# A hybrid decoder layer on one core: modulation rows reduced in one pass over 2048 weights instead of two passes over 1024, with their buffers in pools of their own

## The chip, the core and the metric

The kernel runs on one core of a Trainium2 chip. The metric is the device time of one launch in microseconds. Time before: 1536.57 us, the median of three runs (1535.98 to 1537.61).

Five engines work side by side, each through its own instruction list in order: PE (TensorE) multiplies matrices, DVE (VectorE) and ACT (ScalarE) work on elements, POOL (GpSimd) starts some loads, SP (SyncE) starts nearly all of them. An instruction that waits holds up everything behind it on its engine.

## The reference, cut to what matters

One layer, 256 positions, width 2048, all in float32:

```python
mod = (silu(c) @ ada_w + ada_b)                       # 2048 x 12288 weights, one row of c
sh1, sc1, g1, sh2, sc2, g2 = split(mod, 6)
h = rms_norm(x, norm1_g) * (1 + sc1) + sh1
u, lru_gate, q, k, v, mix_gates = split(h @ w_in + b_in, SPLITS)
y_lru  = rg_lru(causal_conv(u)) * gelu(lru_gate)
y_attn = sliding_window_attention(q, k, v, sinks)
merged = sigmoid(gA) * (y_lru @ w_lru_out) + sigmoid(gB) * (y_attn @ w_attn_out)
x = x + g1 * (merged @ w_o)
h2 = rms_norm(x, norm2_g) * (1 + sc2) + sh2
gate, up = split(h2 @ w_ffn_in, 2)
x = x + g2 * ((silu(gate) * up) @ w_ffn_out)
out = rms_norm(x, final_g)
```

The change concerns the first line: six vectors of 2048 numbers, the *modulations*, each number the product of the row silu(c) with one column of ada_w.

## The kernel before

**The products.** All large products are made by `Item`s in one long list. An item is one 512 KB piece of weights (128 x 1024). Its weights are loaded by SP into a tile `raw` (L313), ACT rounds them to a high part `hi` (L330), DVE subtracts that from `raw` to get the low part `lo` (L342), and PE makes twelve matmuls of 512 columns from them (L382 to L384: high by high, low of the weights by high, high by low of the activations). There are 650 items. `step(i)` writes the instructions for one item: it issues the load of item i+5, the `hi` of item i+3, the `lo` of item i+2 and then the matmuls of item i. There are three buffers for `lo` (N_LO = 3), so the `lo` of item i+2 can start only when PE has done with the `lo` of item i-1, and PE never has more than three items ready.

**The order of the work.** Items run slab by slab: 116 items for the input projection in three pieces (`wi`), then the branch gates (`wgl`), the recurrent branch's output projection (`wl`, items 148 to 179), the other gates (`wga`), attention's output projection (`wa`, items 212 to 243), the output projection (`wo`, items 244 to 275, eight to a slab), then the feed-forward layer (`fg`, `fu`, `f..`, `pf..`). Between the items stand two kinds of smaller work. *Posts* take a slab's sums out of PSUM. *Sides* are generators that a small cost model (`run_sides`, with `charge` and a modelled `clock`) advances while it reckons that DVE and ACT have time: the modulations (`ada`), the norm of the activations (`hmod`), and the two mixers (`mix`: the recurrent unit `lru` and `attention`, four groups each). A side is also advanced at once, whatever the cost model says, where its result is needed: `of` calls `force` until the wanted part of the mixers' result stands, and `ada_to(*ms)` makes all remaining columns of the named modulations. What is written at such a place stands in DVE's list as one block.

**The modulations before.** `crow` holds silu(c) on every partition, in two tiles of 1024. For each block of 128 modulation numbers there is a row tile of 2048 weights to each of 128 partitions, loaded in two halves of 512 KB (`aw`, L503). One DVE instruction (L532, a multiply with a sum along the row) reduces each half; the second half starts from the sum of the first. There are 95 such blocks (the 96th is made by PE at the start), 190 loads and 190 passes. `Halves` holds the loads: two buffers of its own (N_ADA), and further spare tiles from the common pool `bp`, up to five (N_SPARE), where the mixers leave room. The blocks are taken in the order scale 1 and shift 1, gate 1 (m = 2), scale 2 (m = 4), shift 2 (m = 3), gate 2 (m = 5). Before the last `wo` slab, `load_rows(3)` calls `ada_to(3, 4)`; gate 2 may be made as late as the fifth slab of the feed-forward layer, where `all_modulations` calls `ada_to(5)`.

**Buffers.** The common pool `bp` has 37 tiles of 4 KB a partition: 25 counted as `b4` room, 8 for the activations `h`, 2 for `aw`, 2 for `crow`. All temporaries come from it: the mixers' tiles, `lw` (the recurrent unit's weights), and the feed-forward layer's `wx`, `wy` and `v`, which belong to its quads (seven products in place of eight).

Of the kernel before, what the change touches and what calls it, by code (L numbers as in the profile page):

```python
# [9 lines left out]
F32 = mybir.dt.float32  # L10
# [32 lines left out]
AHEAD, N_HI, N_LO, N_ADA, N_B4 = 6, 4, 3, 2, 25  # L43

N_H, N_C = 8, 2
# [32 lines left out]
N_SPARE = 5  # L78

# [4 lines left out]
def hybrid_layer(  # L84
# [11 lines left out]
    dp = ctx.enter_context(tc.tile_pool(name="dp", bufs=1, space=bass.MemoryType.DRAM))  # L96

# [72 lines left out]
    crow = [bp.tile([P, CH], F32, tag="b4", name=f"crow{j}") for j in range(N_C)]  # L170

    def crow_of(i):
        return crow[i // 2][:, i % 2 * 512:(i % 2 + 1) * 512]
# [253 lines left out]
    def seven(loads, block, by_k, act, bank, begin, end, post=None):  # L427
# [24 lines left out]
        def second(i):  # L452
# [4 lines left out]
            y = bp.tile([P, CH], F32, tag="b4", name="wy")  # L457
# [27 lines left out]
    class Halves:  # L485


        def __init__(self, srcs):
            self.srcs, self.got, self.n, self.own = srcs, [], 0, 0
            self.spare, self.limit, self.ahead = lambda: False, len(srcs), AHEAD_T  # L490

        def fetch(self):
            while self.n < min(len(self.srcs), self.limit) and clock["dma"] < clock["pe"] + self.ahead:
# [11 lines left out]
                self.got.append((t, kind, load_time(CH)))  # L505
# [4 lines left out]
        def take(self):  # L510
            t, kind, _ = self.got.pop(0)
            if kind == "own":
                self.own -= 1
            else:
                free(b4=1)
# [4 lines left out]
    def ada_cols(todo, halves):  # L520

        yield 0, 0
        for group in todo:
            for j in range(2):
                for m, kt in group:
                    v = V_ADA + m * NK + kt
                    dst = modc[:, m, kt:kt + 1]
                    if not halves.got:
# [1219 lines left out]
```

## Time and profile before

| what | value |
|---|---|
| median of three runs | 1536.57 us (1535.98 to 1537.61) |
| profiled execution: span from its first to its last instruction | 1534.3 us |
| its own time, taken as the span and 2.3 us around it (1536.57 less 1534.3) | 1536.6 us |
| PE busy | 1519.6 us, 99% of the span |
| DVE busy | 1365.7 us, 89% |
| ACT busy | 880.3 us, 57% |
| mean granted TensorE clock | 0.998 |
| DVE passes over modulation rows, L532 | 190, 241.6 us busy (120.5 + 121.1) |
| bytes moved | 444.58 MB, mean 290 GB/s |

How to read it: each engine's busy time is set against the span. Where one engine is busy nearly all the time, the span is that engine's work and its idle time; what another engine does shows in the time only as idle time of the first. In the views of instructions, a row gives start, duration, engine, line, operation, the output tile and the inputs by name, the size, and in brackets the idle time of the engine just before it with what ended it. Matmuls overlap, so PE's pace is read from the distance between two starts, not from a row's duration. "L342" is a line of the kernel before.

### The profile page before, as it was taken

The page shows a single profiled execution, that of the slowest core. Times are in us where ns is not written, and L with a number is a line of the kernel's source. Part 1 is how long each engine was busy: PE and PEld are TensorE (multiplying, and loading weights), DVE is VectorE, ACT ScalarE, POOL GpSimd, SP SyncE. Part 2 cuts the span into 40 slices and gives each one's busy share as a digit, 9 for nine tenths or more (in the row PEclk, how much of TensorE's full clock was granted, in tenths as well). Part 3 has the DMA queues.
Part 4 walks back from the last instruction along what each step waited for, and adds up shares of the span by engine and source line. Part 5 has one row for each costly group of instructions (what it writes and reads, how often), then busy time and mean ns, then how long its engine had stood idle before and what let it go on. Part 6 is the DMA issues. An engine that isn't in the chain of part 4 may idle for free.

```text
span 1534.3 us, 20203 instructions
## 1 busy us (share of the span) xinstructions
PE 1519.6 (99%) x6851; PEld 1247.3 (81%) x6851; DVE 1365.7 (89%) x1835; ACT 880.3 (57%) x1142; POOL 163.1 (11%) x232
## 2 busy tenths in 40 slices
PE   8999999999999999999999999999999999999997
PEld 5888888888888787888888878888888888888886
DVE  7999999888898887988988899999999999888988
ACT  4654444886964445434445656656566556664664
POOL 0000000000000000000002231034212122321200
PEclk9999999999999999999999999999999999999999
DMA  9999998656787888999999998589988879989983
GB/s 370 377 346 363 348 314 298 210 182 220 239 278 238 280 316 277 362 329 337 375 374 355 335 334 272 162 250 335 278 270 248 268 244 305 281 257 297 274 270 124
DMA packets 138296, 444.58 MB, mean 290 GB/s; under 512 B 16048, under 2 KB 16208, under 8 KB 138192
## 3 DMA queue, kind: packets, MB, share of 16 engines
q1 hardware_dynamic: 112912, 384.02, 70.6%
q0 software_dynamic: 24992, 58.75, 16.0%
q8 instruction: 53, 0.87, 0.2%
q10 hardware_dynamic: 288, 0.52, 0.1%
q14 instruction: 51, 0.42, 0.1%
HBM read 439.02 MB, written 4.21 MB: 289 GB/s over the span
## 4 chain that ended last, share of the span: by engine, by line
PE 92%; DMA 4%; DVE 2%; issue 1%; ACT 1%; SPq 0%; DVEq 0%; ACTq 0%
PE pf L1391 10%; PE f L384 6%; PE f L383 6%; PE f L382 6%; PE wi L383 6%; PE wi L382 6%; PE wi L384 6%; PE wgl L383 2%; PE wl L382 2%; PE wl L384 2%; PE wga L384 2%; PE wga L382 2%; PE wl L383 2%; PE wgl L384 2%; PE wo L383 2%; PE wga L383 2%
## 5 line engine op out<-in xcount | busy, mean ns | idle before, releaser
L330 ACT CAST hi<-raw 128x1024 fp32r<-128x1024 f32 (+1 forms) x540 | 532.1, 996 | 420.3 <-PE wi L384 89.8
L342 DVE TENSOR_TENSOR lo<-raw,hi 128x1024 fp32r<-128x1024 f32 (+1 forms) x540 | 612.0, 1149 | 82.6 <-issue 38.3
L383 PE MATMUL wi<-lo,h 128*128 128x512 f32 x432 | 168.9, 391 | 2.0 <-DVE lo L342 2.0
L382 PE MATMUL wi<-hi,h 128*128 128x512 f32 x432 | 170.6, 395 | 0.0
L384 PE MATMUL wi<-hi,h 128*128 128x512 f32 x432 | 168.8, 391 | 0.0
L382 PE MATMUL f<-hi,h 128*128 128x512 f32 x406 | 158.8, 391 | 0.0
L383 PE MATMUL f<-lo,h 128*128 128x512 f32 x406 | 158.2, 390 | 0.0
L384 PE MATMUL f<-hi,h 128*128 128x512 f32 x406 | 158.1, 389 | 0.0
L532 DVE CUSTOM_DVE_ANT_0 aw<-aw,crow,vec 128x1024 f32<-128x1024 f32 x95 | 120.5, 1277 | 3.4 <-DMA aw<-in_ada_t_dram 3.3
L532 DVE CUSTOM_DVE_ANT_0 aw<-aw,crow,modc 128x1024 f32<-128x1024 f32 x95 | 121.1, 1278 | 1.0 <-DMA aw<-in_ada_t_dram 0.9
L330 ACT CAST hi<-wy 128x1024 fp32r<-128x1024 f32 x55 | 58.0, 1055 | 73.7 <-PE f L384 31.7
L383 PEld LDWEIGHTS wi<-lo,h 128*128 128x128 f32 x432 | 81.6, 189 | 19.7 <-DVE lo L342 2.8
L384 PEld LDWEIGHTS wi<-hi,h 128*128 128x128 f32 x432 | 81.5, 189 | 17.1
L342 DVE TENSOR_TENSOR lo<-wx,hi 128x1024 fp32r<-128x1024 f32 x55 | 67.2, 1222 | 31.5 <-issue 27.6
L382 PEld LDWEIGHTS wi<-hi,h 128*128 128x128 f32 x432 | 81.5, 189 | 16.7 <-ACT acc L611 0.2
L330 ACT CAST hi<-wx 128x1024 fp32r<-128x1024 f32 x55 | 58.0, 1055 | 63.0 <-PE pf L1391 24.0
L383 PEld LDWEIGHTS f<-lo,h 128*128 128x128 f32 x406 | 76.3, 188 | 15.9 <-DVE lo L342 0.3
L384 PEld LDWEIGHTS f<-hi,h 128*128 128x128 f32 x406 | 76.2, 188 | 15.8
L382 PEld LDWEIGHTS f<-hi,h 128*128 128x128 f32 x406 | 76.2, 188 | 15.6
L447 POOL DMA_DIRECT2D wx<-in_w_f_dram x78 | 69.7, 967 | 86.2 <-DMA wx<-in_w_f_dram 84.8
L443 POOL DMA_DIRECT2D wx<-in_w_f_dram x78 | 45.0, 636 | 278.7 <-DVE lo L342 94.6
L342 DVE TENSOR_TENSOR lo<-wy,hi 128x1024 fp32r<-128x1024 f32 x55 | 67.2, 1222 | 6.9 <-ACT hi L330 4.2
(347 smaller groups left out, 3088.6 us busy)
## 6 DMA issues: line engine op xcount, KB each, us to landing
aw<-in_ada_t_dram SPq DMA_DIRECT2D x190, 512.0 KB, 7.2
raw<-in_w_in_dram SPq DMA_DIRECT2D x164, 512.0 KB, 5.4
raw<-in_w_f_dram SPq DMA_DIRECT2D x137, 512.0 KB, 6.7
wx<-in_w_f_dram POOLq DMA_DIRECT2D x156, 256.0 KB, 8.2
raw<-in_w_f2a_dram SPq DMA_DIRECT2D x36, 512.0 KB, 6.1
raw<-in_w_lru_dram SPq DMA_DIRECT2D x32, 512.0 KB, 4.4
raw<-in_w_att_dram SPq DMA_DIRECT2D x32, 512.0 KB, 5.8
raw<-in_w_o_dram SPq DMA_DIRECT2D x32, 512.0 KB, 8.3
```

The costliest lines, as they stand in the source:

```text
L330: nc.scalar.copy(hi[:, cs], live[i][0][:, cs])
L342: nc.vector.tensor_tensor(lo[:, cs], raw[:, cs], f32(hi[:, cs]), op=ALU.subtract)
L382: nc.tensor.matmul(ps, lhsT=lh, rhs=rh, start=start, stop=False, skip_group_check=True)
L383: nc.tensor.matmul(ps, lhsT=lh, rhs=rl, start=False, stop=False, skip_group_check=True)
L384: nc.tensor.matmul(ps, lhsT=ll, rhs=rh, start=False, stop=stop, skip_group_check=True)
L443: nc.gpsimd.dma_start(x[:, j * 512:(j + 1) * 512], block(0, 1))
L447: nc.gpsimd.dma_start(got["x"][:, j * 512:(j + 1) * 512], block(j, j), accum_op=ALU.add)
L532: nc.vector.tensor_tensor_reduce(out=r, in0=r, in1=crow[j], op0=ALU.mult, op1=ALU.add, scale=1.0, scalar=dst if j else vec[:, v:v + 1], ac ...
L1391: nc.tensor.matmul(bank(t, n), lhsT=l[:, rows(t)], rhs=w[:, c0:c0 + 512], start=kt == 0 and k == 0, stop=kt == (EARLY - 2 if (t, n) == (1, ...
```

## The change

- `crow` becomes one tile of 2048. A modulation row is loaded whole, 1 MB in one transfer, and reduced by one DVE instruction of 2048 elements. 95 loads and 95 passes take the place of 190 and 190.
- The rows have tiles of 8 KB a partition. A pool `rows` holds three (one is `crow`, two are for rows), and a pool `early` one more row until the third piece of the input projection begins. Spare tiles of the common pool are no longer used, so at most three rows, then two, are loaded ahead, where before it was up to seven halves. The common pool shrinks from 37 to 29 tiles.
- When the third piece begins, `early` is closed, and `lw` (two tiles for the recurrent unit's weights) is opened in its place.
- When all modulations are made, `lw` and `rows` are closed, and a pool `late` of eight 4 KB tiles is opened in their place. The quads' `wx`, `wy` and `v`, and some tiles of the last feed-forward slabs, come from it. Since the program text that uses `late` must stand behind the last row, `load_rows(3)` now calls `ada_to(3, 4, 5)`: all of gate 2 is made before the last `wo` slab.
- The mixers get less room, and the cost model sees other costs, so the sides are placed elsewhere.

The core of the diff:

```diff
-AHEAD, N_HI, N_LO, N_ADA, N_B4 = 6, 4, 3, 2, 25
+AHEAD, N_HI, N_LO, N_ADA, N_B4 = 6, 4, 3, 2, 21
-N_H, N_C = 8, 2
+N_H, N_EARLY = 8, 1
-N_SPARE = 5
...
-    bp = ctx.enter_context(tc.tile_pool(name="bp", bufs=N_B4 + N_H + N_ADA + N_C))
+    bp = ctx.enter_context(tc.tile_pool(name="bp", bufs=N_B4 + N_H))
...
+    def open_pool(kind, bufs):
+        guard = tc.tile_pool(name=kind, bufs=bufs, side="right", reuse_waits="tile")
...
+    open_pool("rows", N_ADA + 1)
+    open_pool("early", N_EARLY)
...
-    class Halves:
+    class Rows:
         def __init__(self, srcs):
-            self.srcs, self.got, self.n, self.own = srcs, [], 0, 0
-            self.spare, self.limit, self.ahead = lambda: False, len(srcs), AHEAD_T
+            self.srcs, self.got, self.n = srcs, [], 0
+            self.most = {"rows": N_ADA, "early": N_EARLY}
+            self.limit, self.ahead = len(srcs), AHEAD_T
         def fetch(self):
-                if self.own < N_ADA:
-                    t = bp.tile([P, CH], F32, tag="b4", name=f"aw{self.n}")
-                    self.own += 1
-                    kind = "own"
-                elif self.spare():
-                    t = b4(f"aw{self.n}", F32, (CH,))
-                    kind = "b4"
-                else:
+                kind = next((k for k, n in self.most.items() if n > 0), None)
+                if kind is None:
                     return
+                self.most[kind] -= 1
+                t = wide(kind, f"aw{self.n}")
                 nc.sync.dma_start(t, self.srcs[self.n])
...
-            for j in range(2):
-                for m, kt in group:
-                    yield CH * T_DVE + 0.1, 0, 0, 0, halves.here
-                    r = halves.take()
-                    nc.vector.tensor_tensor_reduce(
-                        out=r, in0=r, in1=crow[j], op0=ALU.mult, op1=ALU.add, scale=1.0,
-                        scalar=dst if j else vec[:, v:v + 1], accum_out=dst,
-                    )
             for m, kt in group:
+                yield D * T_DVE + 0.1, 0, 0, 0, wrows.here
+                r = wrows.take()
+                nc.vector.tensor_tensor_reduce(
+                    out=r, in0=r, in1=crow, op0=ALU.mult, op1=ALU.add, scale=1.0,
+                    scalar=vec[:, v:v + 1], accum_out=dst,
+                )
...
+        close_pool("lw")
+        close_pool("rows")
+        open_pool("late", 2 * (N_ADA + 1 + N_EARLY))
...
             if i == N_PIECES - 1:
                 sides[:0] = mix
-                halves.spare = lambda: False
+                del wrows.most["early"]
+                room["b4"] += 2 * N_EARLY
+                close_pool("early")
+                open_pool("lw", 2 * N_EARLY)
...
-                ada_to(3, 4)
+                ada_to(3, 4, 5)
...
-            x = got["x"] = bp.tile([P, CH], F32, tag="b4", name="wx")
+            x = got["x"] = late("wx")
...
-    fetch_to(2)
+    fetch_to(1)
     begin.load(0)
-    fetch_to(6)
+    fetch_to(3)
     begin.load(1)
```

The instructions that this puts in other places, at three places of the program. Names carry the program's own numbers: `lo270` is the low part of item 270, `aw90` is the row with the number 90 (before: the half row), the digits behind the underscore are a buffer's number. The lines are those of the kernel in question: L342, L532 and L1073 before are L360, L544 and L1086 in the changed one. The 128x1 row behind each pass (it hands over the sum) is left out.

DVE before, at the start of the last `wo` slab (items 268 to 275), where PE is about to begin item 268:

```order
L342 TENSOR_TENSOR lo270_6815<-raw270_6746,hi270_6788 128x1024
L532 ISA aw175_6771,modc_162<-aw175_6771,crow0_108,vec_74 128x1024
L1073 TENSOR_TENSOR xr2_6642<-xr2_6642,yo2_6808 128x1024
L342 TENSOR_TENSOR lo271_6841<-raw271_6765,hi271_6813 128x1024
L342 TENSOR_TENSOR lo272_6862<-raw272_6786,hi272_6839 128x1024
L532 ISA aw176_6792,modc_162<-aw176_6792,crow1_109,modc_162 128x1024
```

The same place on DVE in the changed kernel:

```order
L544 ISA aw88_6483,modc_167<-aw88_6483,crow_114,vec_80 128x2048
L1084 TENSOR_TENSOR yo2_6557<-wo2_0_0_6401,g11_5882 128x512
L1084 TENSOR_TENSOR yo2_6557<-wo2_0_1_6402,g11_5882 128x512
L360 TENSOR_TENSOR lo270_6564<-raw270_6497,hi270_6536 128x1024
L544 ISA aw89_6540,modc_167<-aw89_6540,crow_114,vec_80 128x2048
L544 ISA aw90_6568,modc_167<-aw90_6568,crow_114,vec_80 128x2048
L544 ISA aw91_6571,modc_167<-aw91_6571,crow_114,vec_80 128x2048
L544 ISA aw92_6574,modc_167<-aw92_6574,crow_114,vec_80 128x2048
L544 ISA aw93_6577,modc_167<-aw93_6577,crow_114,vec_80 128x2048
L544 ISA aw94_6580,modc_167<-aw94_6580,crow_114,vec_80 128x2048
L1086 TENSOR_TENSOR xr2_6399<-xr2_6399,yo2_6557 128x1024
L360 TENSOR_TENSOR lo271_6608<-raw271_6516,hi271_6562 128x1024
```

Between `lo270` and `lo271` stand six passes of 2048 where one pass of 1024 stood; the fourteen half passes that came behind `lo271` before (176 to 189) are gone from there.

SP's loads at that place in the changed kernel (`xr3` is x's rows for the last slab, `x1d` a store):

```order
L518 DMA aw88_6483<-in_ada_t_dram 128x2048
L518 DMA aw89_6540<-in_ada_t_dram 128x2048
L331 DMA raw273_6560<-in_w_o_dram 128x1024
L1064 DMA xr3_6566<-in_x_r_dram 128x2x512
L518 DMA aw90_6568<-in_ada_t_dram 128x2048
L518 DMA aw91_6571<-in_ada_t_dram 128x2048
L518 DMA aw92_6574<-in_ada_t_dram 128x2048
L518 DMA aw93_6577<-in_ada_t_dram 128x2048
L518 DMA aw94_6580<-in_ada_t_dram 128x2048
L331 DMA raw274_6604<-in_w_o_dram 128x1024
```

(Rows for `raw270` to `raw272` between the first two are left out.) Before, each `aw` load here had a `raw` load between it and the next. With two buffers, the load of `aw90` waits for the pass over `aw88`, that of `aw91` for the pass over `aw89`, `aw92` for `aw90`, `aw93` for `aw91`, `aw94` for `aw92`.

DVE at the recurrent unit's last group (its result's low part is `yl3`, which PE first needs in item 154), before:

```order
L342 TENSOR_TENSOR lo147_3794<-raw147_3723,hi147_3768 128x1024
L835 TENSOR_TENSOR yl3_3785<-uc3_3245,yh3_3784 128x1024
L342 TENSOR_TENSOR lo148_3815<-raw148_3744,hi148_3792 128x1024
L532 ISA aw85_3764,modc_162<-aw85_3764,crow1_109,modc_162 128x1024
L342 TENSOR_TENSOR lo149_3843<-raw149_3766,hi149_3813 128x1024
```

and in the changed kernel:

```order
L360 TENSOR_TENSOR lo154_3812<-raw154_3749,hi154_3791 128x1024
L544 ISA aw45_3662,modc_167<-aw45_3662,crow_114,vec_80 128x2048
L360 TENSOR_TENSOR lo155_3833<-raw155_3769,hi155_3810 128x1024
L360 TENSOR_TENSOR lo156_3854<-raw156_3789,hi156_3831 128x1024
L852 TENSOR_TENSOR yl3_3848<-uc3_3433,yh3_3847 128x1024
L360 TENSOR_TENSOR lo157_3878<-raw157_3808,hi157_3852 128x1024
```

`yl3` moved from behind `lo147` to behind `lo156`, that is from seven items ahead of its first use to the place where `force` demands it. (The pass over `aw46` behind `yl3` is left out.)

More of the change, by code (lines that the diff above doesn't have):

```diff
@@ L169, in hybrid_layer @@
     early_root()
-    crow = [bp.tile([P, CH], F32, tag="b4", name=f"crow{j}") for j in range(N_C)]
+    crow = wide("rows", "crow")
     def crow_of(i):
-        return crow[i // 2][:, i % 2 * 512:(i % 2 + 1) * 512]
+        return crow[:, i * 512:(i + 1) * 512]
     c_ps = []
@@ L968, in post @@
                 free(b4=8)
-                halves.spare = lambda: len(halves.got) - halves.own < N_SPARE and not h2 and (
-                    len(at_lo) == 4 or used["b4"] + 4 <= room["b4"]
-                )
             gated(banks, gl[s])
@@ L1231, in f_parts @@
         if not seven_:
-            fh, fl = b4(f"fh{s}", F32R), b4(f"fl{s}", F32R)
+            new = late if s == 9 else b4
+            fh, fl = (new(f"f{p}{s}", F32R, (4, S)) for p in "hl")
             yield from parts_of(pts, fh, fl)
@@ L1670, in hybrid_layer @@
     until({(0, 2), (1, 2)})
-    fetch_to(14)
+    fetch_to(7)
     begin.post(2)
@@ L1678, in hybrid_layer @@
     clock.update(pe=T_START[0], dve=T_START[1], act=T_START[1])
[L1679 to L1681 removed]
+    wrows.limit, wrows.ahead = len(wrows.srcs), AHEAD_T
+    streams.append(wrows)
     sides.extend((hmod, ada))
```

60 lines of the change are left out of this document (32 added, 28 removed).

## The prediction

> **What bounds the kernel now.** I read the page's busy times and its chain first, then the table of windows, then PE's waits.
>
> ```profile
> PE 1519.6 (99%) x6851; PEld 1247.3 (81%) x6851; DVE 1365.7 (89%) x1835; ACT 880.3 (57%) x1142; POOL 163.1 (11%) x232
> PE 92%; DMA 4%; DVE 2%; issue 1%; ACT 1%; SPq 0%; DVEq 0%; ACTq 0%
> ```
>
> PE is busy for all but 14.7 us (1534.3 less 1519.6), and the chain that ended last is PE for 92%. The change leaves PE's matmuls alone, so the time after it is PE's work, 1519.6 us, and whatever idle time PE then has. Where the 14.7 us lie:
>
> ```profile
> 0.00:50.00 50.00, 45.01 (x191) 31.70 (x192) 39.05 (x72) 23.04 (x37) 0.70 (x6) 0.97 0.99 379
> 150.00:200.00 50.00, 50.00 (x222) 41.42 (x221) 47.05 (x67) 23.69 (x28) 0.00 (x0) 1.00 0.95 345
> 800.00:850.00 50.00, 49.61 (x241) 41.41 (x240) 44.01 (x70) 29.46 (x47) 9.66 (x14) 1.00 1.02 352
> 850.00:900.00 50.00, 49.93 (x224) 40.89 (x223) 43.11 (x65) 27.70 (x37) 14.41 (x20) 1.00 1.03 342
> 900.00:950.00 50.00, 49.61 (x219) 39.86 (x218) 46.54 (x57) 30.43 (x37) 14.38 (x20) 1.00 0.98 296
> 1500.00:1550.00 50.00, 25.87 (x137) 22.22 (x135) 26.84 (x45) 13.16 (x22) 0.00 (x0) 0.94 0.24 83
> ```
>
> The columns are the stretch, its length, the busy times of PE, PEld, DVE, ACT and POOL, PE's clock, the share of the DMA engines and GB/s. The first 50 us cost 5.0 us of idle time, the end 8.4 (34.3 less 25.87), which the change doesn't touch, and everything between about 1.3. So there is hardly anything to win; what counts is whether PE, which is never short of work now, runs dry somewhere. PE's waits on DVE are small:
>
> ```profile
> PE wi L383 <- DVE lo L342: 2.0, 2, 1.8
> PE fr L383 <- DVE lo L342: 0.3, 2, 0.2
> ```
>
> The 1.8 us wait is the price list for a stall, since it shows what follows one:
>
> ```profile
> 38.44 0.50 PE L383 MATMUL wi<-lo,h 128*128 128x512 f32 x1 [1.81 <-DVE lo L342]
> ...
> 36.60:38.40 1.80, 0.03 (x1) 1.00 1.02 407
> 38.40:40.00 1.60, 1.56 (x5) 0.65 1.02 399
> 40.00:42.10 2.10, 2.10 (x6) 0.50 1.02 410
> 42.10:45.00 2.90, 2.90 (x14) 0.97 1.03 404
> ```
>
> After 1.81 us of idleness the granted clock (the third number from the end) falls to about half until 42.1: of the 3.7 us from 38.4 about half, 1.8 us, are lost. I charge each stall of this size or longer with 1.8 us more.
>
> **How far PE can run without DVE.**
>
> ```profile
> 819.73 0.39 PE L384 MATMUL wo<-hi,ml 128*128 128x512 f32 x1
> ...
> 823.13 0.39 PE L384 MATMUL wo<-hi,ml 128*128 128x512 f32 x1
> ```
>
> Between these starts lie 15 matmuls' steps: 3.40 / 15 = 0.227 us a matmul, 2.72 us an item of twelve. With three `lo` buffers PE has at most three items ready when DVE turns to something else: 8.2 us, and 0.2 for the one matmul of the fourth item that needs no `lo`, 8.4 us.
>
> **Part 1: one pass for two.**
>
> ```profile
> L532 DVE CUSTOM_DVE_ANT_0 aw<-aw,crow,modc 128x1024 f32<-128x1024 f32 x95 | 121.1, 1278 | 1.0 <-DMA aw<-in_ada_t_dram 0.9
> L532 DVE CUSTOM_DVE_ANT_0 aw<-aw,crow,vec 128x1024 f32<-128x1024 f32 x95 | 120.5, 1277 | 3.4 <-DMA aw<-in_ada_t_dram 3.3
> L342 DVE TENSOR_TENSOR lo<-raw,hi 128x1024 fp32r<-128x1024 f32 x469 | 564.4, 1219 | 77.2 <-issue 37.7 <-ACT hi L330 18.0 <-PE wl L383 3.7
> L342 DVE TENSOR_TENSOR lo<-raw,hi 128x512 fp32r<-128x512 f32 x71 | 48.8, 687 | 5.4 <-PE f L383 4.0 <-issue 0.6 <-PE pf L1391 0.5
> ```
>
> A pass of 2048 isn't in the trace. DVE's subtraction grows by 532 ns for 512 elements, 1.04 ns each; 1278 ns and 1024 more elements make 2.34 us (it cannot cost more than two passes, 2.56). Saved: 95 x 0.2 = 21 us at most of DVE's busy time; but passes overlap their neighbours by 0.07 us, so nearer 95 x 0.14 = 13 us. PE is at 50.00 of 50.00 even where DVE is busiest (150 to 200), so this is hidden behind PE, except for the two `fr` waits: -0.3 us (bounds -0.5 and 0).
>
> **Part 2: the start.** There the DMA engines are the limit (share 0.99), and the bytes come in the same order.
>
> ```profile
> 14.89 1.28 DVE L532 CUSTOM_DVE_ANT_0 aw<-aw,crow,vec 128x1024 f32<-128x1024 f32 x1 [0.65 <-DMA aw<-in_ada_t_dram]
> 16.10 0.16 DVE L1628 RECIPROCAL rc<-rc 128x2 f32<-128x2 f32 x1
> 17.54 1.28 DVE L532 CUSTOM_DVE_ANT_0 aw<-aw,crow,modc 128x1024 f32<-128x1024 f32 x1
> 18.74 0.47 DVE L1647 SCALAR_TENSOR_TENSOR xT<-xT,modc,rx_ps 128x256 f32<-128x256 f32 x1
> ```
>
> The first half starts as it lands, at 14.89. The whole row lands 512 KB later, at 400 GB/s 1.3 us (about 16.2), and is reduced by 18.5. The reciprocal, which stood behind the first half at 16.10, comes 2.4 us later; the second half's pass behind it (1.2 us) is gone. PE's first large products begin 1.2 us later. They run into the wait of 1.81 us shown above, which takes that up. I put 0; bounds -1.8 (the wait gets too short to cost the clock) and +1.2 (its `lo` comes later as well).
>
> **Part 3: the recurrent unit's last group.** `yl3` now stands on DVE behind `lo156`, and `lo156` waits until PE has done with `lo153`. From the start of that matmul PE has four steps to the first that reads `yl3` (0.9 us); DVE needs the matmul's end (0.4), the subtraction's pace of 1.14 and 1.22 for `yl3`, and some 0.1 to notice:
>
> ```profile
> 432.89 1.21 DVE L342 TENSOR_TENSOR lo<-raw,hi 128x1024 fp32r<-128x1024 f32 x1
> 434.02 1.21 DVE L835 TENSOR_TENSOR yl<-uc,yh 128x1024 fp32r<-128x1024 f32 x1
> ```
>
> 0.4 + 1.14 + 1.22 + 0.1 = 2.8, less 0.9: PE stands for 1.9 us, as long as the wait at 38.44, so I add 1.8 for the clock. Sum 3.7 (bounds 1.9 and 3.7). The Trainium skill, "TensorE: Matmul & The Clock Gate", part 1, says that the clock is throttled after at least one idle window of about 3.4 us. By that rule these 1.8 us would not be charged; the row at 38.44 speaks against it, as 1.81 us were enough there.
>
> **Part 4: gate 2 ahead of the last `wo` slab.** This decides. I count from T, the moment PE begins item 268. Before, it is the end of this wait on PE:
>
> ```profile
> 799.54 1.22 DVE L342 TENSOR_TENSOR lo<-raw,hi 128x1024 fp32r<-128x1024 f32 x1
> 800.68 0.68 DVE L1071 TENSOR_TENSOR yo<-wo,g 128x512 f32<-128x512 f32 x1
> 801.79 0.69 DVE L1071 TENSOR_TENSOR yo<-wo,g 128x512 f32<-128x512 f32 x1 [0.43 <-PE wo L384]
> 802.40 1.22 DVE L342 TENSOR_TENSOR lo<-raw,hi 128x1024 fp32r<-128x1024 f32 x1
> 803.54 1.28 DVE L532 CUSTOM_DVE_ANT_0 aw<-aw,crow,vec 128x1024 f32<-128x1024 f32 x1
> ```
>
> PE runs dry at T+8.4 unless `lo271` has come. In front of it now stand six whole passes, and with two buffers each load waits for the pass before last. `lo269` starts at about T-2.5 (buffer of `lo266`, one item before T), the pass over `aw88` ends at T+0.9, and `aw90` can be loaded from T+1.0. What a load of 1 MB takes from issue to landing, L, is not in the trace; nearest are those of 512 KB, first in a quiet stretch (300 to 400, median in the last column), then the shortest, median and longest of `raw` from 450 to 550 and of `aw` from 700 to 830:
>
> ```profile
> raw<-in_w_in_dram SPq DMA_DIRECT2D x30, 512.0 KB, 4.1
> aw<-in_ada_t_dram SPq DMA_DIRECT2D x5, 512.0 KB, 5.4
> ...
> DMA to landing us min/median/max: 3.4/4.4/8.0
> ...
> DMA to landing us min/median/max: 5.5/8.9/13.2
> ```
>
> While PE stands, no `raw` load is behind these, so the quiet rows count: 4.1 and 1.3 for another 512 KB at 400 GB/s, L = 5.4 (low 3.4 + 1.3 = 4.7; high 5.4 + 1.3 = 6.7; far end 8.9 + 1.3 = 10.2). `aw90`, with `xr3` ahead of it (0.5), lands at T+1.5+L; pass 2.34; then `aw92` and `aw94`, each load, pass and 0.1 between them, L+2.44. Behind them stand the residual's addition and `lo271`, 1.14 each at DVE's pace and 0.1. Sum: 1.5 + 3L + 2.34 + 4.88 + 2.4 = 3L + 11.1; at L = 5.4 T+27.3. The rows between (`aw89`, `aw91`, `aw93`) fit into the gaps. PE's stall is 27.3 - 8.4 = 18.9 us; with 4.7 and 6.7 it is 16.8 and 22.8, with 10.2 33.3. If the loads cost nothing, six passes back to back from T+3.3 end at T+17.3, and the stall is 11.3. The clock adds 1.8. The Trainium skill, "DMA: Bandwidth & Descriptors", section "Bandwidth", gives 6.15 us for 1 MB, and advises transfers of 1 MiB or more. Put in for L, that would make an estimated stall of 21 us; no run here shows a load of this size.
>
> What waits behind the burst: on SP the loads of items 274 and on. PE needs item 274 three items after it resumes (8 us), and `raw274` is issued right behind `aw94`'s load, L + 2.3 + 2.4, or 10 us, before PE resumes: covered.
>
> What is gone in return: fourteen half passes between 805 and 905, beside PE's work; nothing but the `fr` waits. Elsewhere (items 160 to 268) two buffers leave 3 to 5 items, 8 to 14 us, from a buffer's release to its next pass. Against 10.2 us that means waits of a few us on DVE, within PE's reserve: 0 (bound +2). The quads' loads in `late` are issued 16 items, 44 us, ahead of their use: 0, within the same bound.
>
> **Sum.** -0.3 + 0 + 3.7 + 18.9 + 1.8 + 0 = +24.1 us on the profiled execution's own 1536.6 (its span of 1534.3 and 2.3 around it, which is the median too): **1560.7 us**.
>
> **The rivals.**
>
> *The burst is bound by DVE alone.* If 1 MB lands much faster than I take it, the stall tends to 11.3: 1549.3 to 1554.8 with the other low ends. Against it: each load's issue waits for a pass. 0.12.
>
> *The loads are as slow as in the busy stretch*, L = 10.2: stall 33.3, 24.1 + 14.4 more, 1575 us. For it: 8.9 is the median at this very place; against it: SP has nothing else to load then. 0.10.
>
> *A short stall leaves the clock alone.* The `fr` waits of up to 0.2 us did so: the clock is 1.00 in the row of 900 to 950. If the 1.9 us in part 3 count with those, its 1.8 us for the clock go, and the time is 1558.9. Against it: 1.81 us at 38.44 were enough. 0.12. This is also what the rule of the Trainium skill quoted in part 3 would make of it.
>
> *Faster: DVE was what held PE up.* Place: the waits on `lo`, 2.0 + 0.3, and the clock's 1.8 behind the longest; the relief of 13 us ends them: 1536.6 - 4.1 = 1532.5. It decides only if the six passes of the burst hide behind PE's reserve, that is if they take no more than 8.4 us less 5.5 us for DVE's other work from T (0.9 for `aw88`'s end, 1.2 for two `yo`, three more instructions of 1.14); at 2.34 us each one would fit, not six. 0.04 (half of it within 0.2%).
>
> *My forecast*, 1554.8 to 1568.1 by the ends above: 0.62.
>
> **The numbers.** 0.2% of the time, 3 us, is about what a measurement of this kernel can tell from no change. All cases but the last rival are slower by more: slower 0.96, same 0.02, faster 0.02. The range 1550 to 1570 holds the forecast, the clock rival and most of the DVE-bound one, and leaves out the slow loads and the gain.
>
> **What would show it.** PE's waits: one long wait on `lo` in `wo`, 17 to 23 us, in which DVE's row before `lo271` are six passes with idle time ended by DMA `aw`; half clock for some 3.7 us behind it; a wait of about 1.9 us in `wl` on `yl`; passes of 2.3 us. I am wrong if no wait in `wo` exceeds 10 us, if the passes have no waits on DMA between them, or if long waits stand elsewhere.

## The result, and the profile after

| | before | after |
|---|---|---|
| median, same chip | 1536.28 us (1534.85 to 1537.61, 4 runs) | 1560.28 us (1560.01 to 1564.54, 4 runs) |
| ratio to before, 95% interval | | 1.0162 [1.0148, 1.0176] |
| span of the profiled execution | 1534.3 us | 1558.3 us |
| mean TensorE clock | 0.998 | 0.990 |

The change made the kernel 24.0 us slower, in the medians and in the spans. First the busy times on the page of the kernel after, and its DVE group of passes:

```profile
PE 1523.2 (98%) x6851; PEld 1249.8 (80%) x6851; DVE 1356.4 (87%) x1645; ACT 881.2 (57%) x1143; POOL 162.9 (10%) x232
...
L544 DVE CUSTOM_DVE_ANT_0 aw<-aw,crow,vec 128x2048 f32<-128x2048 f32 x95 | 222.8, 2346 | 10.9 <-DMA aw<-in_ada_t_dram 10.7
```

The passes did become cheaper, 222.8 us in place of 241.6, and DVE has 9.3 us less to do. PE has the same 6851 matmuls. It stands idle for 35.1 us (1558.3 less 1523.2) where it was 14.7, and it is busy 3.6 us longer, mostly since more of its matmuls ran at half clock. The table of PE's waits says where it stands idle (engine, line, what it waited for: total, times, longest; the wait for `warm`, which the kernel before has too, is left out):

```profile
PE wo L401 <- DVE lo L360: 19.6, 1, 19.6
PE rx_ps L1645 <- ACT sqx L1643: 2.1, 1, 2.1
PE wl L402 <- DVE yl L852: 1.8, 1, 1.8
...
PE wi L401 <- DVE lo L360: 0.8, 1, 0.8
PE wi L634 <- DVE acc L623: 0.7, 3, 0.3
```

One wait in `wo` holds nearly everything. This is what DVE did ahead of it (start, duration, instruction, in brackets the idle time before it):

```profile
806.84 1.22 DVE L360 TENSOR_TENSOR lo<-raw,hi 128x1024 fp32r<-128x1024 f32 x1
808.37 2.35 DVE L544 CUSTOM_DVE_ANT_0 aw<-aw,crow,vec 128x2048 f32<-128x2048 f32 x1 [0.32 <-DMA aw<-in_ada_t_dram]
...
813.48 2.35 DVE L544 CUSTOM_DVE_ANT_0 aw<-aw,crow,vec 128x2048 f32<-128x2048 f32 x1 [2.75 <-DMA aw<-in_ada_t_dram]
...
815.96 2.35 DVE L544 CUSTOM_DVE_ANT_0 aw<-aw,crow,vec 128x2048 f32<-128x2048 f32 x1
...
820.76 2.35 DVE L544 CUSTOM_DVE_ANT_0 aw<-aw,crow,vec 128x2048 f32<-128x2048 f32 x1 [2.44 <-DMA aw<-in_ada_t_dram]
...
823.45 2.35 DVE L544 CUSTOM_DVE_ANT_0 aw<-aw,crow,vec 128x2048 f32<-128x2048 f32 x1 [0.33 <-DMA aw<-in_ada_t_dram]
...
828.34 2.35 DVE L544 CUSTOM_DVE_ANT_0 aw<-aw,crow,vec 128x2048 f32<-128x2048 f32 x1 [2.54 <-DMA aw<-in_ada_t_dram]
...
831.76 3.64 DVE L360 TENSOR_TENSOR lo<-raw,hi 128x1024 fp32r<-128x1024 f32 x3
```

Six passes stand between `lo270` and `lo271`, and every second one waits for its row: passes 2, 4 and 6 of the block begin at 813.48, 820.76 and 828.34, 7.3 and 7.6 us apart. That is the chain that the prediction described, a load of one row, its pass, and only then the next load into the same buffer. The loads' own view gives the time from issue to landing in this stretch (row tiles, 1 MB each, median in the last column), and PE's rows show when it goes on:

```profile
aw<-in_ada_t_dram SPq DMA_DIRECT2D x7, 1024.0 KB, 5.1
```

```profile
833.03 0.79 PE L401 MATMUL wo<-lo,mh 128*128 128x512 f32 x1 [19.57 <-DVE lo L360]
```

The clock (third number from the end) where it falls and where it rises again; every stretch between reads 0.50:

```profile
818.00:819.00 1.00, 0.00 (x0) 0.00 (x0) 0.32 (x2) 0.00 (x0) 0.00 (x0) 0.82 0.99 418
...
839.00:840.00 1.00, 1.00 (x5) 0.78 (x5) 0.00 (x0) 0.06 (x1) 0.00 (x1) 0.94 1.05 309
```

It is at half from 818.64 to 839.12 (a stretch of 1 us that reads 0.82 was at full speed for 0.64 us), so for 6.1 us after PE resumed, and about half of that, 3.0 us, is lost.

The second place is `yl3`. PE's wait, and the clock while and after it stands:

```profile
462.36 0.39 PE L401 MATMUL wl<-lo,yh 128*128 128x512 f32 x1
464.58 0.50 PE L402 MATMUL wl<-hi,yl 128*128 128x512 f32 x1 [1.83 <-DVE yl L852]
...
465.39 0.40 PE L402 MATMUL wl<-hi,yl 128*128 128x512 f32 x1
```

```profile
464.00:466.00 2.00, 1.42 (x6) 1.18 (x7) 2.00 (x2) 0.00 (x0) 0.00 (x0) 1.00 0.99 406
466.00:468.00 2.00, 2.00 (x11) 1.62 (x10) 1.76 (x3) 0.79 (x1) 0.00 (x0) 1.00 0.88 299
```

The wait is as forecast, the clock stays at 1.00. But a stop costs more than the wait that the table counts: from 462.36 to 465.39 PE makes four steps, 3.03 us in place of 0.91, so 2.12 are lost, 0.29 more than 1.83. (Matmuls overlap: one takes 0.39 us where a step is 0.227, so the last one before the stop takes 0.16 more than its step, and the step behind the first one after it is 0.34.)

To see where along the program time is lost, I take PE's first matmul of a stage in both traces and compare the distances. The table has all kernels of the experiments too (differences to before in us, of one profiled execution each, the spans taken to 0.1 us; the first column ends with the first transposition through `ident`, which before begins at 229.53 us):

| kernel | start | to first `wo` | `wo` to first `fg` | `fg` to the end | sum |
|---|---|---|---|---|---|
| after | +0.2 | +3.2 | +22.3 | -1.6 | +24.0 |
| 1 passes sooner from the 41st on | +1.8 | +9.3 | +0.5 | -1.9 | +9.7 |
| 2 last rows not loaded | +0.1 | +4.7 | +15.8 | -1.9 | +18.7 |
| 3 before, gate 2 forced | +0.1 | +0.1 | +20.9 | -2.0 | +19.1 |
| 4 slack of 8 | +0.2 | +54.8 | -0.4 | -1.9 | +52.7 |
| 5 spread from `lo155`, forced late | +0.8 | +4.9 | -0.4 | -1.7 | +3.7 |
| 6 the same, mixers sooner | +0.4 | +11.9 | -0.4 | -1.4 | +10.5 |
| 7 three rows forced | +0.3 | +7.9 | +9.4 | -1.9 | +15.6 |
| 8 forced late only | +0.5 | +3.2 | -0.3 | +9.3 | +12.7 |
| 9 spread, forced late, `yl3` sooner | 0.0 | +1.0 | -0.4 | -1.7 | -1.2 |
| 10 spread from `lo158`, forced late | +0.4 | +4.7 | -0.4 | -1.7 | +3.2 |

### The profile page after: what moved, and what is told of

The parts are those of the page before. It is cut to its first block, busy times and chain, and to the rows that moved or that the text cites. A ratio compares the mean times of both kernels' runs of the same rounds, so it can differ in the third digit from the quotient of the medians.

```text
span 1558.3 us, 19844 instructions
## 1 busy us (share of the span) xinstructions
PE 1523.2 (98%) x6851; PEld 1249.8 (80%) x6851; DVE 1356.4 (87%) x1645; ACT 881.2 (57%) x1143; POOL 162.9 (10%) x232
## 4 chain that ended last, share of the span: by engine, by line
PE 67%; DMA 1%; DVE 1%; issue 0%; ACT 0%; DVEq 0%; ACTq 0%
PE pf L1405 9%; PE f L402 6%; PE f L400 6%; PE f L401 6%; PE wga L402 2%; PE wga L400 2%; PE wga L401 2%; PE wa L402 2%; PE wa L400 2%; PE wa L401 2%; PE wo L401 2%; PE wo L402 2%; PE wo L400 2%; PE wl L402 2%; PE wl L400 2%; PE wl L401 2%
## 5 line engine op out<-in xcount | busy, mean ns | idle before, releaser
L360 DVE TENSOR_TENSOR lo<-raw,hi 128x1024 fp32r<-128x1024 f32 (+1 forms) x540 | 611.5, 1150 | 108.8 <-ACT hi L348 28.9
L544 DVE CUSTOM_DVE_ANT_0 aw<-aw,crow,vec 128x2048 f32<-128x2048 f32 x95 | 222.8, 2346 | 10.9 <-DMA aw<-in_ada_t_dram 10.7
L360 DVE TENSOR_TENSOR lo<-wx,hi 128x1024 fp32r<-128x1024 f32 x55 | 67.2, 1223 | 36.0 <-issue 30.6
L360 DVE TENSOR_TENSOR lo<-wy,hi 128x1024 fp32r<-128x1024 f32 x55 | 67.2, 1222 | 7.2 <-ACT hi L348 4.4
L1405 PE MATMUL pf<-hi,fc 128*128 128x512 f32 x256 | 71.0, 389 | 0.0
```

The source lines that it names most:

```text
L360: nc.vector.tensor_tensor(lo[:, cs], raw[:, cs], f32(hi[:, cs]), op=ALU.subtract)
L544: nc.vector.tensor_tensor_reduce(out=r, in0=r, in1=crow, op0=ALU.mult, op1=ALU.add, scale=1.0, scalar=vec[:, v:v + 1], accum_out=dst,)
L1405: nc.tensor.matmul(bank(t, n), lhsT=l[:, rows(t)], rhs=w[:, c0:c0 + 512], start=kt == 0 and k == 0, stop=kt == (EARLY - 2 if (t, n) == (1, ...
```

## The experiments

The theory: the block of six passes at the last rows of x, with its chain of loads over two buffers, is the loss, and the late `yl3` most of the rest. The rivals: wide passes and loads as such cost time wherever they stand; the pools that open and close are what is waited for; the loads don't matter in the block, only DVE's time. The kernel before was measured beside each group of experiments and took 1535.29, 1536.33 and 1535.41 us there, so times of different groups are compared by their distance to it.

### 1 and 5: the block taken away, two ways

The cost model decides how early a pass is placed. The first kernel has it reckon with 0.8 us for a pass in place of 2.36 once 40 rows are done.

```diff
-                yield D * T_DVE + 0.1, 0, 0, 0, wrows.here
+                yield (D * T_DVE + 0.1 if len(cols_done) < 40 else 0.8), 0, 0, 0, wrows.here
```

> The changed kernel, with the planner charged 0.8 us for a pass in place of 2.36 from the 41st on, so that it places the rows some items sooner: the last pass then stands behind lo261 and none are left to be forced at the last rows of x; the same 95 passes, loads, buffers and pools. Theory (the forced run of six passes and its chain of loads is the loss): the wait of 19.6 us on lo before the last weights of wo goes, and the 2.8 us of half clock behind it, while the wait on yl of 1.8 stays: 1560.3 - 22.4 = 1537.9 us, between 1536 and 1541, since a pass more in wa can make lo late by some tenths here and there. Rival 1 (wide passes and loads as such cost the time, wherever they stand; the six are only where it shows): the wait goes, but the same passes stall TensorE in wa and wo piece by piece: 1548 or more. Rival 2 (the pools that open and close are what waits): nothing moves, 1560.

Measured: 1543.89 us against 1535.29, ratio 1.0057 [1.0044, 1.0069]. The wait in `wo` is gone, and 15.4 of the 24 us with it, so neither the pools nor the wide passes as such made it. But the kernel is 8.6 us above the one before where the theory gave 1.6, and the table shows where the 7 us lie: 9.3 us are lost between 230 us and the first `wo`. DVE and PE in one window, first of the changed kernel, then of this one (columns as in the prediction: length, busy PE, PEld, DVE, ACT, POOL):

```profile
350.00:450.00 100.00, 100.00 (x452) 83.31 (x451) 89.28 (x106) 72.08 (x94) 0.00 (x0) 1.00 0.73 248
```

```profile
350.00:450.00 100.00, 96.02 (x427) 78.16 (x426) 94.85 (x112) 66.10 (x89) 0.00 (x0) 1.00 0.77 279
```

And its waits there:

```profile
PE wgl L401 <- DVE lo L360: 4.0, 4, 1.8
...
PE wl L401 <- DVE lo L360: 1.6, 2, 1.3
```

The passes went to where the mixers already fill DVE: 94.85 us busy of 100. A pass between two `lo` is harmless only while DVE gets through its list in time. The six waits add up to 5.6 us, with 0.29 for each stop 7.3. With 1.0 that the kernels without such waits lose there too (the ninth), that leaves 1.0 of the 9.3 unassigned.

The fifth kernel therefore charges the lower price only from `lo155` on, where all of `yl` was thought to be made, and forces the last gate not at the last rows of x but where the program first asks for a tile of the pool `late`:

```diff
+        if "late" not in pools:
+            ada_to(5)
         return pools["late"][1].tile([P, *shape], dt, tag="b4", name=name)
...
-                yield D * T_DVE + 0.1, 0, 0, 0, wrows.here
+                yield (D * T_DVE + 0.1 if at["lo"] < 155 else 0.8), 0, 0, 0, wrows.here
...
-                ada_to(3, 4, 5)
+                ada_to(3, 4)
```

> The changed kernel with two edits: the planner charges 0.8 us for a pass in place of 2.36 from lo155 on (after the last yl, not from the 41st pass as in the first try), and the last gate is forced only where the first tile of the late pool is asked for, not at the last rows of x. The passes then stand one every two or three items up to lo276, and none are forced. Theory (the forced run costs 22.4 us; the first try lost 6 us of that again because VectorE was booked too full between 350 and 550 us, where the wait on yl is decided): the forced wait and its half clock go, no new waits come in wl and wgl, the wait of 1.8 us on yl stays, and a few passes after wo give back some of the feed-forward's relief: 1560.3 - 22.4 + 0.5 = 1538.4 us, 1536.5 to 1541. Rival (a wide pass beside the work costs some time anywhere, 8 KB loads against weights): again 1543 or more, with waits in wl, wga or wa.

Measured: 1541.34 us against 1536.33, ratio 1.0034 [1.0023, 1.0046]; the profiled execution was the shortest of its six runs. There are no waits on `lo` in `wgl`, `wga`, `wa` or `wo`. Of the rest, one wait is the largest:

```profile
PE wl L404 <- DVE yl L854: 3.6, 1, 3.6
```

On DVE the reason stands right ahead of it:

```profile
458.94 2.34 DVE L546 CUSTOM_DVE_ANT_0 aw<-aw,crow,vec 128x2048 f32<-128x2048 f32 x1
...
462.35 2.34 DVE L546 CUSTOM_DVE_ANT_0 aw<-aw,crow,vec 128x2048 f32<-128x2048 f32 x1
...
465.76 1.22 DVE L854 TENSOR_TENSOR yl<-uc,yh 128x1024 fp32r<-128x1024 f32 x1
```

A second cheap pass slipped in ahead of `yl3`, which in the changed kernel starts at 463.31. So both attempts missed for the same reason, a pass put ahead of something that PE was already short of.

### 2: what the loads are worth in the block

The rows 90 to 94 are not loaded, and their passes run over the tile of row 89 (so the kernel leaves out five blocks of 128 numbers of the feed-forward's gate).

```diff
+                if self.n >= 90:
+                    self.n += 1
+                    self.got.append((self.last, None, clock["pe"]))
+                    continue
                 kind = next((k for k, n in self.most.items() if n > 0), None)
...
-                t = wide(kind, f"aw{self.n}")
+                t = self.last = wide(kind, f"aw{self.n}")
```

> The changed kernel, but the last five rows (numbers 90 to 94) are not loaded: their passes run over the tile of row 89, so five columns of the feed-forward's gate come out of the wrong numbers; every pass stands where it stood. Theory (two buffers make the loads of the forced run wait for its passes, so that the chain load, pass, load sets its length): VectorE does the six passes back to back, and the wait on lo falls from 19.6 to about 11.3 us (the prediction's value for VectorE alone), with some 2 to 2.8 us of half clock behind it: 1560.3 - 8.3 = 1552.0 us, 1550.5 to 1553. Rival (VectorE's passes alone set the length, the loads are hidden): 1560. Second rival (the stall is below what the gate of the clock notices when it is shorter): 1549.

Measured: 1555.27 us against 1535.29, ratio 1.0127 [1.0114, 1.0141]. The block's first and last pass on DVE, and PE behind it:

```profile
811.32 2.35 DVE L548 CUSTOM_DVE_ANT_0 aw<-aw,crow,vec 128x2048 f32<-128x2048 f32 x1 [1.75 <-DMA aw<-in_ada_t_dram]
...
823.30 2.35 DVE L548 CUSTOM_DVE_ANT_0 aw<-aw,crow,vec 128x2048 f32<-128x2048 f32 x1
```

```profile
827.99 0.79 PE L401 MATMUL wo<-lo,mh 128*128 128x512 f32 x1 [13.05 <-DVE lo L360]
```

Back to back, the six passes end in 14.3 us, and PE waits 13.05: the prediction's 11.3 for DVE alone and the 1.75 us for which row 89, which is still loaded, was late. Against 19.57 the chain of loads is worth 6.5 us of the wait. The time is 3 us above the 1552 expected; 1.75 of it is that wait for row 89, and in this execution `yl3`'s wait did halve the clock for 3.4 us, which is 1.7 us more. The rival, DVE alone, falls.

### 3: the old kernel with gate 2 forced

One part of the change alone, put into the kernel before:

```diff
-                ada_to(3, 4)
+                ada_to(3, 4, 5)
```

> The kernel before, with one part of the change alone: the last group of modulations (the feed-forward's gate) is forced at the last rows of x as in the changed kernel, in passes of 1024 over 4 KB loads with the old pools and buffers: some 15 half passes stand there together. Theory (that the rows have to end there is the loss, not the width or the pools): about 15 x 1.28 = 19.2 us of VectorE in place of 14.1, with up to seven loads ahead of it, so the wait on lo is 16 to 20 us, half clock 2 to 3 us behind it, and 1 to 1.7 us come back in the feed-forward, whose VectorE no longer has passes: 1536.3 + 16.4 + 2.8 - 1.5 = 1554 at the middle, 1551 to 1558. Rival (8 KB rows and two buffers are what makes the stall): the narrow loads run ahead and the stall is short: 1540 to 1545.

Measured: 1555.31 us against 1535.29, ratio 1.0126 [1.0112, 1.014]. The wait, and the clock behind it:

```profile
827.99 0.79 PE L383 MATMUL wo<-lo,mh 128*128 128x512 f32 x1 [17.69 <-DVE lo L342]
```

```profile
829.00:831.00 2.00, 2.00 (x6) 1.60 (x5) 1.30 (x2) 1.05 (x2) 1.48 (x3) 0.50 1.09 178
831.00:833.00 2.00, 2.00 (x9) 1.54 (x9) 0.69 (x1) 0.00 (x0) 0.00 (x0) 0.85 1.04 278
```

Without one wide pass, 8 KB tile or new pool, 19.1 of the 24.0 us are there, with the same 2 us back in the feed-forward. Most of the loss is the place where the gate must be ready. What width and two buffers add is small here, 4 us of 24 in the medians with `yl3`'s wait among them, since fewer passes were left over (six rows in place of 15 half rows).

### 7 and 8: how the wait depends on the block

Seven is the changed kernel with the lower price from `lo155` on alone (the middle edit of 5), which leaves three rows to force. Eight is the changed kernel with the later place alone (the first and last edit of 5), which leaves four, at another place.

> The changed kernel with only the planner's price at 0.8 us from lo155 on: three passes are left to be forced behind lo271 in place of six. Theory (chain of loads, pass by pass): the wait ends where the third pass of the six ended, so it is shorter by 828.34 - 815.96 = 12.4 us: 19.6 - 12.4 = 7.2 us, with 2 to 3 us of half clock still behind it: 1560.3 - 12.4 = 1547.9 us, 1546 to 1550. Rival (the wait is set by VectorE's passes alone, three times 2.4 less): wait 12.5 us, 1553. Rival on the clock (a wait of 7 us is too short to halve it): 1545.

Measured: 1549.5 us against 1536.33, ratio 1.0087 [1.0073, 1.0101].

```profile
PE wo L401 <- DVE lo L360: 6.7, 1, 6.7
PE wl L402 <- DVE yl L852: 4.0, 1, 4.0
```

The block's wait is 6.7 us where the chain gave 7.2 and DVE's passes alone 12.5. The lower price again put a pass ahead of `yl3`, 2.2 us more there, and this time half clock.

> The changed kernel with one edit: the last gate is forced where the first tile of the late pool is asked for, not at the last rows of x, with the planner's prices as they were. Two of the six passes then go in beside the feed-forward's first items, and four are forced together behind lo288, two of them with their row already there. Theory: PE's reserve of three items, 8.4 us, takes most of 4 x 2.4 us and of a chain of two loads; the wait is 2 to 6 us instead of 19.6, with 2 us of half clock: 1560.3 - 22.4 + 6 = 1544 us, 1541 to 1548. Rival (what is forced costs the same wherever it stands): four of six, 15 us: 1555.

Measured: 1550.22 us against 1536.33, ratio 1.0094 [1.0078, 1.0109], 6 us more than expected and 5 less than the rival gave. The last two of the four passes on DVE, then PE:

```profile
866.36 2.35 DVE L546 CUSTOM_DVE_ANT_0 aw<-aw,crow,vec 128x2048 f32<-128x2048 f32 x1 [2.74 <-DMA aw<-in_ada_t_dram]
...
869.88 2.35 DVE L546 CUSTOM_DVE_ANT_0 aw<-aw,crow,vec 128x2048 f32<-128x2048 f32 x1 [1.16 <-DMA aw<-in_ada_t_dram]
```

```profile
874.36 0.79 PE L403 MATMUL fu<-lo,h 128*128 128x512 f32 x1 [8.00 <-DVE lo L362]
```

The wait is 8.0 us where 2 to 6 were expected. The chain is the same one: 3.9 us of waiting for rows between the passes, with the two rows ahead used up at once. So a later place alone isn't enough; the passes must not be left over.

### 4 and 6: room for the mixers

Four raises the cost model's third slack, for passes and mixers alike; six is the kernel of 5 with a slack of 3 us more for the mixers alone, until `lo157`.

```diff
-SLACK = (2.0, 2.0, 3.0)
+SLACK = (2.0, 2.0, 8.0)
```

> The changed kernel with the planner's third slack at 8 in place of 3: it lets mixers and passes run up to 8 us over the end of an item from the last piece of the first product on. The last pass then stands behind lo204 and yl3 behind lo132 instead of lo156. Theory: neither the forced run (19.6 + 2.8) nor the wait on yl (1.8) is left; relief in the feed-forward stays: 1560.3 - 24.2 = 1536.1 us. Rival: a slack that lets VectorE be booked beyond the item makes lo late in wl and wga, and TensorE waits there instead: three to ten waits of 0.5 to 2 us, 1540 to 1548.

Measured: 1588.59 us against 1535.29, ratio 1.0339 [1.0323, 1.0354], the slowest of all, further off than the rival. Its largest wait, and the window:

```profile
PE wi L634 <- DVE acc L623: 19.7, 18, 3.6
```

```profile
240.00:350.00 110.00, 94.98 (x413) 76.89 (x412) 105.50 (x130) 69.15 (x104) 0.00 (x0) 0.93 0.80 307
```

DVE has no block and no late `yl3` any more, and the kernel is 53.3 us slower than the one before, where the changed one is 24.0 slower. In `wi` PE hands its sums to DVE, which is 105.5 of 110 us busy, and gets them back late, 18 times.

```diff
+                more = 3.0 if at["lo"] < 157 and s is not ada and s is not hmod else 0
-                if max(clock["dve"], clock["pe"]) + s.cost[0] > end + clock["slack"]:
+                if max(clock["dve"], clock["pe"]) + s.cost[0] > end + clock["slack"] + more:
...
-                if max(clock["act"], clock["pe"]) + s.cost[1] > end + clock["slack"] or not s.advance():
+                if max(clock["act"], clock["pe"]) + s.cost[1] > end + clock["slack"] + more or not s.advance():
```

> The last kernel with a third edit: up to lo157 the planner may run the mixers (not the passes) 3 us further over the end of an item, so that yl3 stands behind lo131 in place of lo157. Theory (the wait on yl is a mixer placed too late, since fewer temporaries are free): the wait of 1.8 us goes, nothing else moves: 1538.4 - 1.8 = 1536.6 us, 1534.5 to 1538.5. Rival: the mixers are then what makes lo late between 300 and 400 us, as the slack of 8 did: 1539 to 1546, with waits on lo or acc there.

Measured: 1546.59 us against 1536.33, ratio 1.0069 [1.0056, 1.0081]. The rival holds. The wait on `yl` is gone, but mixers moved in among the last pieces of `wi` cost more than it did:

```profile
PE wi L637 <- DVE acc L626: 7.9, 12, 3.5
```

### 10 and 9: one edit each from the fifth

Ten is the kernel of 5 with 158 in place of 155.

> The fifth run's kernel with one edit, the lower price of a pass from lo158 on in place of lo155, so that no pass is added ahead of yl3. Theory (two passes more ahead of yl3 made its wait 3.6 instead of 1.8 us): the wait is 1.8 us again: 1541.3 - 1.8 = 1539.5 us, 1538 to 1541. Rival (the wait on yl is hidden in part, as TensorE's clock stays full behind it): no change, 1541.3.

Measured: 1539.31 us against 1535.41, ratio 1.0027 [1.0016, 1.0038]. That is 3.9 us above the kernel before, where the fifth is 5.0 above it: 1.1 us less, not the 1.8 expected, and the two intervals overlap, so the times alone don't decide between the theory and its rival. The trace shows what became of the wait: it is 1.83 us in place of 3.64, the changed kernel's own to the hundredth. But here the clock falls behind it, as it did in neither of the other two:

```profile
464.86 0.50 PE L404 MATMUL wl<-hi,yl 128*128 128x512 f32 x1 [1.83 <-DVE yl L854]
```

```profile
466.00:467.00 1.00, 1.00 (x5) 0.77 (x4) 1.00 (x2) 0.00 (x0) 0.00 (x0) 0.57 1.04 426
...
469.00:470.00 1.00, 1.00 (x4) 0.75 (x4) 0.37 (x1) 0.56 (x1) 0.00 (x0) 0.73 0.97 385
```

Nine adds the mixers' slack only where it doesn't reach `wi`:

```diff
+                more = 3 if 130 <= at["lo"] < 157 and s in mix else 0
```

(used in the two lines as in 6.)

> The kernel with the passes spread and forced late (as in the fifth run), with two edits: the lower price of a pass holds from lo158 on, after the last yl, and between lo130 and lo157 the planner may run mixers 3 us further, which puts yl3 behind lo154 (lo157 in the changed kernel) and moves no mixer before that. Theory: the wait on yl (3.6 us in the fifth run) goes to under 0.5 us, no acc waits as in the sixth run: 1541.3 - 3.4 = 1537.9 us, 1536 to 1540. Rival (yl3 isn't the cause of what the fifth run still lost, the start is): 1540 to 1542.

Measured: 1535.62 us (11 runs) against 1535.41 (17 runs), ratio 1.0 [0.9991, 1.0009]. `yl3` now starts 7 us earlier than in the changed kernel:

```profile
456.27 1.22 DVE L855 TENSOR_TENSOR yl<-uc,yh 128x1024 fp32r<-128x1024 f32 x1
```

PE's waits between 60 and 800 us are four of 0.3 us or less, and the wide passes, the pools and the early end of the modulations are all still there. So the 24 us came from where some instructions stand, put there by the planner or forced, and the wide passes cost nothing that a measurement to 0.1% shows. Nor do they bring anything: DVE's busy time is 1355.8 us against 1365.7 before, and the kernel takes as long as before. None of the kernels tried is faster than the one before.

## Why the prediction was right

Forecast +24.1, measured +24.0; the terms agree less well than the sum.

- **Part 1** (-0.3). A pass takes 2.346 us (2.34 worked out). The saving is hidden behind PE, but the feed-forward gave back 1.6 us, not 0.3: I counted only the waits named `fr`. Gaps of a few tenths that the table of waits doesn't list go as well when no passes stand there any more. That this comes from the passes being gone, not from their width, shows in the third experiment: the old kernel's `fg` to the end is 2.0 us shorter too.
- **Part 2** (0, bounds -1.8 and +1.2). Measured +0.2 at 230 us. The first large products begin 2.0 us later and the wait of 1.81 us with its half clock is gone, as the lower bound described; in exchange PE waits 2.1 us at `rx_ps`, which I did not foresee, and behind that wait the clock is at half from 19.93 to 23.35 us. In the other kernels' profiled executions this part varies from 0.0 to +1.8.
- **Part 3** (3.7 = 1.9 + 1.8). The wait is 1.83. The 1.8 for the clock was not lost in the profiled execution of the changed kernel, and was lost in the second and tenth kernels' behind the same wait. So that term is one of chance, and neither I nor the rival that leaves the clock alone had it right; the last section shows what decides it. What else was lost ahead of `wo` comes to 1.3 us: 0.29 for the stop, and 1.0 that the ninth kernel loses there too (the `acc` waits are part of it).
- **Part 4** (18.9). Measured 19.6, for the stated cause. T is 804.9: item 268's first matmul begins at 804.91, and PE runs dry at 813.46, so the reserve is 8.55 us where I had 8.4. SP's row shows the five loads, each held up by the pass ahead of it:

```profile
805.75 17.73 SPq L518 DMA_DIRECT2D aw<-in_ada_t_dram x5
```

  `aw90` is issued at T+0.8 and its pass begins at T+8.6, 1.7 us later than reckoned, as this first load took some 7.7 us beside `xr3` and the last `raw`. The two steps of the chain took 7.3 and 7.6 us against 7.84, which gives 0.8 back, and the longer reserve 0.15. The second and seventh kernels bear the formula out at other ends: 13.05 with the loads gone, 6.7 for half the block.
- **The clock behind it** (1.8). Measured 2.7 (22.3 less 19.6), since the half clock went on for 6.1 us after PE resumed, not for 3.7. (The half clock alone costs 3.0 and the stop 0.3; six of the kernels without this block are 0.3 to 0.4 us faster than before in this stage, which hides a part.) This is a term mis-sized, not a step that failed.
- **Waits on rows elsewhere** (0). Right: of the passes' 10.7 us of waiting for rows 8.4 lie in the block (the five waits of the fence above), the rest in two places, and no other wait of PE on `lo` stands behind 60 us.

Sum of what was measured: +0.2 + 3.2 + 19.6 + 2.7 - 1.6 = +24.1, with 0.1 of rounding. The errors (feed-forward -1.3, clock in part 3 -1.8, the rest ahead of `wo` +1.3, clock in part 4 +0.9, wait +0.7, start +0.2) nearly cancel, so a hit within 0.5 us is luck; the 19.6 us are not. The rival that counted on DVE alone is refuted by the second kernel, that of slow loads by the 5.1 us. The Trainium skill, "DMA: Bandwidth & Descriptors", section "Bandwidth", has 6.15 us for 1 MB; the rows of the quiet block, issue to landing, have a median of 5.1, so the estimate of 21 us of stall by it was too high.

## What to carry to other kernels

Where one engine is busy 99% of the time, as here, cheaper work on another engine gained nothing (the ninth kernel), and what counted was which deadlines the change moved: a pool that opens late turned "any time in the next 35 items or so" into "now", and the third experiment, one line in the old kernel, shows that alone to cost 19 to 20 us. A block that must be done at once costs its length less the reserve that the bound engine has (three items, 8.55 us here), and with two buffers its length is that of the chain load, pass, load. When work is spread out again, look at where the helping engine has room: the same passes cost 7 us between 350 and 480 us (DVE up to 95% busy) and nothing from there on.

## What the runs showed of the hardware

**The clock changes in steps of 3.41 us.** From the 1 us stretches, the half clock lasted 3.42 us behind the wait at 38.44 of the kernel before (38.86 to 42.28), 3.40 in the tenth (466.14 to 469.54), 6.82 in the seventh (465.60 to 472.42) and 20.48 in the kernel after (818.64 to 839.12): one, one, two and six times 3.41. The edges in the kernel before:

```profile
38.00:39.00 1.00, 0.56 (x2) 0.52 (x3) 1.00 (x3) 1.00 (x2) 0.00 (x0) 0.93 1.06 410
...
42.00:43.00 1.00, 1.00 (x5) 0.78 (x5) 1.00 (x2) 0.00 (x0) 0.00 (x0) 0.86 1.05 408
```

Waits of 1.81 to 2.11 us halved the clock in some executions and left it alone in others, behind the same instruction; the fifth kernel's 3.6 us left it alone, the seventh's 4.0 did not. What decides is where a wait falls. Within one execution all falls lie on one grid of 3.413 us: in the fourth kernel's they come at 260.41, 294.55, 311.61, 349.16, 383.29, 427.67 and 461.80, which is 10, 5, 11, 10, 13 and 10 steps apart. Cut along its grid (its one fall, at 1533.62 us behind the last product, lies 313 steps behind 465.24), the fifth kernel's wait is shared by two windows, with 1.85 and 1.79 us of idle time (the window less PE's busy time, the second number behind it), and the clock (third number from the end) stays:

```profile
461.83:465.24 3.41, 1.56 (x7) 0.95 (x6) 3.41 (x4) 1.48 (x2) 0.00 (x0) 1.00 0.87 293
465.24:468.66 3.42, 1.63 (x7) 1.37 (x8) 1.74 (x2) 0.00 (x0) 0.00 (x0) 1.00 1.02 422
468.66:472.07 3.41, 3.41 (x17) 2.83 (x16) 2.61 (x2) 1.06 (x1) 0.00 (x0) 1.00 1.00 412
```

In the seventh 2.72 of the 4.0 us fall into one window, and the next one runs at half:

```profile
462.18:465.59 3.41, 0.69 (x4) 0.23 (x2) 3.41 (x4) 1.05 (x1) 0.00 (x0) 1.00 0.89 332
465.59:469.01 3.42, 2.14 (x5) 1.76 (x6) 1.22 (x2) 0.00 (x0) 0.00 (x0) 0.50 1.05 436
```

The changed kernel's 1.83 us at `yl3` were shared by two windows, 0.91 and 0.92, and the tenth's lay in one. So it goes in all twelve profiled executions: the 29 windows at full clock with 1.93 us or more of idle time were each followed by one at half, of the ten with 1.79 to 1.85 four were, and none with 1.78 or less. At half clock, a window with 0.73 us or more idle was followed by another at half, one with 0.27 or less by full speed. That is why the block's half clock outlasted its wait by 6.1 us: PE resumed 0.73 us into a window that began at 832.30, and had to work through one more. The Trainium skill, "TensorE: Matmul & The Clock Gate", Part 1, "What's actually happening", describes a window of 3413 ns that runs freely and isn't set back when a kernel starts. The grid and its steps agree with that. Its rule that one idle window throttles is not what these runs show: a window with 1.81 us idle was enough in the kernel before, and PE worked for the rest of it. Why windows of 1.79 to 1.85 us go either way stays open; the ends of matmuls are modelled in the profile, which makes these figures uncertain.
